# Hybrid decoder step: values of four heads in one 512-column product, gates feature-major, output projection over four open banks

## The chip, the cores and the metric

The kernel runs on one core of a Trainium2 chip. The metric is the device time of one execution in microseconds (us). Times below come from three timed runs and from one profiled execution, whose trace has every instruction of the engines: PE (TensorE, the matmuls), DVE (VectorE), ACT (ScalarE), POOL (GpSimd), and SP, which issues most DMA transfers.

## The reference, cut to what matters

One layer over 2048 prompt tokens, 16 meta tokens and 8 single-token samples, model width 1024, float32. After an RMS norm one projection with 2560 columns gives the S5 input u (512), and for four heads of 128 the query q, forget logit, value and gate (512 columns each):

```python
hn = rms_norm(h, norm_mix_g)
z = hn @ w_in                      # u | q | f | i (values) | g (gates)
y5 = s5_mix(u, ...)                # complex scan, GELU, GLU
# per head, in chunks of 64 tokens:
o = qd @ S + att @ v               # att = mask(qd @ kd^T)
S = diag(decay) @ S + kd'^T @ v
o = o * rsqrt(mean(o * o) + EPS)   # over the head's 128 columns
o = o * norm_g * silu(g)
h = h + concat([y5, o]) @ w_out
h = h + conv_ffn(rms_norm(h, norm_ffn_g), ...)
```

## The kernel before, in words

The prompt is cut into four blocks b = 0 to 3 of 512 tokens. Block 0 also carries 24 extra columns (meta tokens and samples), so its feature-major products run in two column ranges of 256 and 280. Every matrix product is made of three passes over operands split in two (`wh`, `wl` for weights, `ah`, `al` for activations): high by high, high by low, low by high. A weight unit of 1024 columns per partition is loaded into `st` (two buffers), `w_unit`; ACT copies its high part (L449) and DVE subtracts for the low one (L83); `wh` and `wl` have three buffers.

`fm_mm` (L480) makes feature-major results: weights stationary, 512 tokens wide, 24 matmuls for 128 features. `tm_mm` (L500) makes token-major results: 128 tokens stationary, 256 weight columns wide, 24 matmuls for 256 columns. `ex_mm` (L514) does the extra tokens of block 0, 16 matmuls for 256 columns.

For each block `head(b, a, h)` runs four times: the forget gate f by `fm_mm`, a chain on DVE (L612, L615, the scans L622, the reciprocal L632 and products), q by `fm_mm`, then value and gate of this head together by `tm_mm` (four row tiles, two weight units, evicted by ACT at L670 and L671), the scores (L690, masked at L693), turned keys (L696, L698), the state products (L701, L710), the outputs `po` (L713, L714), their squares on ACT (L720), the inverse root on DVE and POOL (L520, L521), a normalisation times gate on DVE for each of four row tiles (L723), four PE turnings (L726) and an ACT copy with the norm weight into `mixh` (L732).

Between the heads of block b stand S5 tiles of block b-1, `s5(b-1, ...)`, eight a block: table load L832, input products L847, rotations and scans L885 on DVE, output products L896 and L899, and after every second tile the GELU and turning (L814, L818). Block 3 has S5 tiles 0 to 3 of block 2 with head 0 and 4 to 7 with head 1, and its own with heads 2 and 3. Behind the heads come `u_proj(b)`, and for the block before it the GLU, the split of `mixh` and `out_proj`, in four column groups of 256: two weight units, 96 matmuls, addition of the residual x and a store to `h_d`. The feed-forward part follows after block 3.

The order of instructions on each engine is fixed at build time by the framework's scheduler; it may place code of one function inside another. PSUM banks come from three pools: `bank` with three for products, `gbank` with three for the heads, and two for turnings and S5.

Of the kernel before, what the change touches and what calls it, by code (L numbers as in the profile page):

```python
# [37 lines left out]
def kernel(  # L38
# [563 lines left out]
    def head(b, a, h):  # L602
# [49 lines left out]
        wu = []  # L652
        for kq in range(2):
            st = w_stage()
            for j in range(2):
                dma_w(st.rearrange("p (k j c) -> p k j c", k=4, j=2)[:, :, j],
                      ap(win, kq * 512 * 2560 + 1536 + 128 * h + 512 * j,
                         [[2560, 128], [128 * 2560, 4], [1, 128]]))
            hi, lo = split_w(st, 1024)
            wu.append((v3(hi, 4, 256), v3(lo, 4, 256)))  # L660
        v = hgp.tile([128, 4, 128], F32, name="hv")
        g = hgp.tile([128, 4, 128], F32, name="hg")
        for t2_ in range(2):
            p = v3(bank(), 2, 256)
            o = None
            for i in range(2):
                t = 2 * t2_ + i
                o = tm_mm(p[:, i, :], wu, (4, 4),
                          lambda ai, k: a[ai][:, k, t * 128:t * 128 + 128], o)
            ACT(v[:, 2 * t2_:2 * t2_ + 2], p[:, :, 0:128], AF.Copy)  # L670
            ACT(g[:, 2 * t2_:2 * t2_ + 2], p[:, :, 128:256], AF.Silu)  # L671
        if b == 0:
            pe = bank()
            ex_mm(pe[:, :256], wu, (4, 4), E["stat"], 104)
            t = ex_sum(pe, 40, 64, 256)
            ie = exa.tile([40, 256], F32, name="ie")
            add(ie, pe[:40, :256], t)
            ge = exa.tile([40, 128], F32, name="ge")
            ACT(ge, ie[:, 128:256], AF.Silu)
# [42 lines left out]
        for t in range(4):  # L722
            stt(g[:, t, :], po[:, t, :], r[:, t:t + 1], g[:, t, :], op0=OP.mult, op1=OP.mult)  # L723
        px = v3(gbank(), 4, 128)
        for t in range(4):
            nc.tensor.transpose(px[:, t, :], g[:, t, :], ident)  # L726
        if b % 2:
            mh = E["mxp"].tile([128, BT], F32, name="mixh", bufs=4)
        else:
# [245 lines left out]
    def out_proj(b, m, between=None):  # L975
# [4 lines left out]
        for q in range(4):  # L980
            if between is not None:
                between(q)
            qs = slice(256 * q, 256 * q + 256)
            wu = [w_unit(wout, 4 * kq, 4, 256 * q, 256) for kq in range(2)]
            xr = v3(x4(), 4, 256)
            dma_w(xr, x_prompt[0, b * BT:b * BT + BT, qs].rearrange("(t p) c -> p t c", p=128))
            for t2_ in range(2):
                p = v3(bank(), 2, 256)
                o = None
                for i in range(2):  # L990
                    t = 2 * t2_ + i
                    o = tm_mm(p[:, i, :], wu, (4, 4),
                              lambda ai, k: m[ai][:, k, t * 128:t * 128 + 128], o)
                add(xr[:, 2 * t2_:2 * t2_ + 2], p, xr[:, 2 * t2_:2 * t2_ + 2])
            dma(h_d[b][:, qs].rearrange("(t p) c -> p t c", p=128), xr)
            if b == 0:
                xe = scr()[:10, :256]
                dma_w(xe[0:8], x_sample.rearrange("n o d -> (n o) d")[:, qs])
                dma_w(xe[8:10], meta_tokens[14:16, qs])
                pe = bank()  # L1000
                ex_mm(pe[:, :256], wu, (4, 4), st, 42)
                t = ex_sum(pe, 10, 32, 256)
                add(t, pe[:10, :256], t)
# [265 lines left out]
```

## Time and profile before

| | us |
|---|---|
| median of three runs (2626.48 to 2635.57) | 2628.86 |
| the profiled execution | 2622.47 |
| its span in the trace | 2620.6 |
| PE busy | 2496.9 |
| DVE busy | 1456.0 |
| ACT busy | 903.6 |
| mixing part (blocks 0 to 3, to 1111.2) | 1111.2 |
| feed-forward part, from there to 2591 | 1479.8 |

Busy times are sums over the span; the engines run side by side. A chain of waits is followed back from the last instruction of a stretch. A product's time in a run is the chain's time divided by its count; the mean duration of one matmul in the groups is longer, since matmuls are pipelined.

### The profile page before, as it was taken

The numbers are of one execution on the slowest core, as the hardware profiler recorded it, in microseconds if no ns is written. First come the engines' busy times: TensorE is split into PE (matmuls) and PEld (weight loads), VectorE is DVE, ScalarE is ACT, GpSimd is POOL, SyncE is SP. The second block draws the span as 40 slices with busy tenths as digits, with TensorE's granted clock in tenths as the row PEclk, the third lists the DMA queues.
The fourth block names the chain that finished last, engine by engine and source line by source line (L and its number), as shares of the span: only waits on it lengthen the run. The fifth ranks groups of instructions, "written<-read, shape, count | busy, mean of one in ns | idle before, by whom it ended". The sixth has DMA issues, their size and how long they took to land.

```text
span 2620.6 us, 39925 instructions
## 1 busy us (share of the span) xinstructions
PE 2496.9 (95%) x16515; PEld 2263.8 (86%) x16515; DVE 1456.0 (56%) x2978; ACT 903.6 (34%) x1564; POOL 166.2 (6%) x254
## 2 busy tenths in 40 slices
PE   7887998999999999999999999999999999999998
PEld 6786876888888888989999999999889898989887
DVE  6875697678669688553333333345843333343344
ACT  3553344434425445341313131223531313131222
POOL 1232100100000001000000000000300000000000
PEclk9997999999999999999999999999999999999999
DMA  4345433553564662731111111111521111111111
GB/s 126 103 138 184 98 111 133 153 167 121 132 197 131 168 219 86 247 92 49 49 45 45 49 48 42 43 47 57 195 73 49 49 49 49 49 49 49 41 48 74
DMA packets 274939, 252.50 MB, mean 96 GB/s; under 512 B 11367, under 2 KB 255999, under 8 KB 270654
## 3 DMA queue, kind: packets, MB, share of 16 engines
q1 hardware_dynamic: 264680, 220.42, 27.9%
q0 software_dynamic: 9904, 29.48, 3.5%
q8 instruction: 129, 2.11, 0.3%
q14 instruction: 52, 0.43, 0.1%
q10 hardware_dynamic: 174, 0.06, 0.0%
HBM read 216.41 MB, written 33.27 MB: 95 GB/s over the span
## 4 chain that ended last, share of the span: by engine, by line
PE 72%; DVE 11%; ACT 4%; DMA 3%; issue 3%; POOL 1%; SPq 0%; POOLq 0%; ACTq 0%; DVEq 0%
PE mm L480 41%; PE mm L500 25%; DVE wl L83 1%; DVE hf L632 1%; PE mm L514 1%; DMA st<-in_w_out_dram 1%; POOL rstd L521 1%; DVE sB L86 1%; DMA st<-in_w_in_dram 1%; PE tp L899 1%; ACT wh L449 1%; DVE sA L885 1%; DVE al L83 1%; PE tp L847 1%; DVE sA L86 1%
## 5 line engine op out<-in xcount | busy, mean ns | idle before, releaser
L480 PE MATMUL mm<-ah,wh 128*128 128x512 f32 (+3 forms) x2320 | 817.6, 353 | 5.1 <-ACT ah L552 3.8
L480 PE MATMUL mm<-al,wh 128*128 128x512 f32 (+3 forms) x2320 | 814.6, 351 | 1.1 <-DVE al L83 1.1
L480 PE MATMUL mm<-ah,wl 128*128 128x512 f32 (+3 forms) x2320 | 814.9, 351 | 0.5 <-DVE wl L83 0.5
L449 ACT ACTIVATE wh<-st 128x1024 fp32r<-128x1024 f32 (+1 forms) x264 | 275.7, 1046 | 859.8 <-PE mm L480 315.5
L480 PEld LDWEIGHTS mm<-ah,wh 128*128 128x128 f32 x2320 | 441.1, 190 | 60.0 <-ACT ah L552 4.5
L480 PEld LDWEIGHTS mm<-ah,wl 128*128 128x128 f32 x2320 | 441.1, 190 | 55.7 <-DVE wl L83 1.0
L480 PEld LDWEIGHTS mm<-al,wh 128*128 128x128 f32 x2320 | 441.0, 190 | 54.6 <-DVE al L83 1.6
L83 DVE TENSOR_TENSOR wl<-st,wh 128x1024 fp32r<-128x1024 f32 (+1 forms) x264 | 318.1, 1206 | 272.6 <-ACT wh L449 271.4
L500 PE MATMUL mm<-wh,gh 128*128 128x256 f32 x1408 | 399.6, 284 | 2.0 <-DVE hacc L80 1.5
L500 PE MATMUL mm<-wh,gl 128*128 128x256 f32 x1408 | 399.5, 284 | 0.0
L500 PE MATMUL mm<-wl,gh 128*128 128x256 f32 x1408 | 399.2, 284 | 0.0
L500 PE MATMUL mm<-wh,ah 128*128 128x256 f32 x1024 | 291.7, 286 | 7.3 <-ACT hg L671 3.2
L500 PE MATMUL mm<-wh,al 128*128 128x256 f32 x1024 | 290.9, 284 | 5.8 <-DVE al L83 5.0
L500 PE MATMUL mm<-wl,ah 128*128 128x256 f32 x1024 | 289.0, 284 | 1.2 <-DVE wl L83 1.2
L80 DVE TENSOR_TENSOR hacc<-hacc,mm 128x512 f32<-128x512 f32 x192 | 131.3, 685 | 267.1 <-PE mm L500 267.0
L500 PEld LDWEIGHTS mm<-wh,gh 128*128 128x128 f32 x1408 | 270.9, 192 | 3.0 <-DVE hacc L80 1.7
L500 PEld LDWEIGHTS mm<-wh,gl 128*128 128x128 f32 x1408 | 270.8, 192 | 0.4
L500 PEld LDWEIGHTS mm<-wl,gh 128*128 128x128 f32 x1408 | 271.0, 192 | 0.0
L500 PEld LDWEIGHTS mm<-wh,ah 128*128 128x128 f32 x1024 | 194.7, 191 | 10.3 <-ACT hg L671 3.4
L500 PEld LDWEIGHTS mm<-wh,al 128*128 128x128 f32 x1024 | 195.2, 191 | 8.4 <-DVE al L83 6.2
L500 PEld LDWEIGHTS mm<-wl,ah 128*128 128x128 f32 x1024 | 194.8, 191 | 2.1 <-DVE wl L83 1.8
L86 DVE TENSOR_TENSOR c<-c,mm 128x512 f32<-128x512 f32 (+1 forms) x110 | 63.7, 579 | 215.6 <-PE mm L480 214.3
(377 smaller groups left out, 2606.0 us busy)
## 6 DMA issues: line engine op xcount, KB each, us to landing
st<-in_ffn_w_up_dram SPq DMA_DIRECT2D x96, 512.0 KB
big<-tab_d SPq DMA_DIRECT2D x32, 1156.0 KB
st<-in_w_in_dram SPq DMA_DIRECT2D x48, 512.0 KB
st<-in_w_in_dram SPq DMA_DIRECT2D x64, 256.0 KB
st<-in_w_out_dram SPq DMA_DIRECT2D x32, 512.0 KB
st<-in_ffn_w_down_dram SPq DMA_DIRECT2D x32, 512.0 KB
x<-in_x_prompt_dram SPq DMA_DIRECT2D x30, 512.0 KB
h_d<-x POOLq DMA_DIRECT2D x16, 512.0 KB, 4.8
```

The lines of the kernel that those rows point to most:

```text
L80: tt_(o, a, b, op=OP.add)
L83: tt_(o, a, b, op=OP.subtract)
L86: tt_(o, a, b, op=OP.mult)
L449: ACT(hi[:, :n], st[:, :n], AF.Copy)
L480: mm(p[:, :n], w[wi][:, k, :], a[ai][:, k, c0:c0 + n], start=(i == 0), stop=(i == 3 * nk - 1))
L500: o = mm(dst, lhs(ai, k), (hi, lo)[wi][:, kk, :], start=(i == 0), stop=(i == tot - 1))
L514: mm(dst[:m], stat[:, k, :m], w[:, kk, :], start=(i == 0), stop=(i == tot - 1))
L521: nc.gpsimd.tensor_tensor(r, r, mhalf[:ss.shape[0], :n], op=OP.pow)
L632: nc.vector.reciprocal(R[:, c0:c1], P[:, c0:c1])
L847: mm(pes[i // ng][:, i % ng, :], Bk[:, i, :], UT[:, i // 2, :nj], start=True, stop=True)
L885: nc.vector.tensor_tensor_scan(out=G[:, i, 1:129], data0=sv[:, RHO, g:g + 1].to_broadcast([128, 128]), data1=xr[:, i, :], initial=Hc[:, g: ...
L899: o = mm(py[:, 2 * i:2 * i + 2, :].rearrange("p a b -> p (a b)"), G[:, 2 * i + j, 0:128], Cm[:, 2 * i + j, :], start=False, stop=(j == 1))
```

## The change

Values and gates of a head are made apart. `v_proj(b)` makes the values of all four heads ahead of the block's first head: `tm_wide` keeps four banks open (two of each pool), one for each row tile of 128 tokens, takes weight units of two row blocks by 512 columns and uses each for 24 matmuls 512 wide before the next. The gate of a head is made feature-major by `fm_mm` and goes through SiLU straight into `mixh`. The normalisation of `po` becomes four ACT copies with a scale, which are turned, and one DVE instruction (L737) multiplies by norm weight and gate. `out_proj` goes through `tm_wide` too, in two groups of 512 columns. Lines of the changed kernel lie further down: L690 becomes L699, L726 becomes L735, L847 becomes L862, L538 becomes L561, L832 becomes L847.

```diff
+    def tm_wide(src, c0, lhs, done, ex=None):
+        pb = [(bank, gbank)[t % 2]() for t in range(4)]
+        pe = bank() if ex is not None else None
+        for i in range(4):
+            wu = w_unit(src, 2 * i, 2, c0, 512)
+            for t in range(4):
+                for kk in range(2):
+                    k = 2 * i + kk
+                    for j, (wi, ai) in enumerate(PASS):
+                        mm(pb[t], lhs(ai, k, t), wu[wi][:, kk, :], start=(k == 0 and j == 0),
+                           stop=(k == 7 and j == 2))
+                if i == 3:
+                    done(t, pb[t])
...
     def head(b, a, h):
...
-                dma_w(st.rearrange("p (k j c) -> p k j c", k=4, j=2)[:, :, j],
-                      ap(win, kq * 512 * 2560 + 1536 + 128 * h + 512 * j,
...
-                o = tm_mm(p[:, i, :], wu, (4, 4),
-                          lambda ai, k: a[ai][:, k, t * 128:t * 128 + 128], o)
-            ACT(v[:, 2 * t2_:2 * t2_ + 2], p[:, :, 0:128], AF.Copy)
-            ACT(g[:, 2 * t2_:2 * t2_ + 2], p[:, :, 128:256], AF.Silu)
...
+        wg = w_unit(win, 0, 8, 2048 + 128 * h, 128)
+        for p, q0, n in fm_mm(wg, a, 8, cols):
+            n_ = min(n, BT - q0)
+            ACT(mh[:, q0:q0 + n_], p[:, :n_], AF.Silu)
...
+        v = E["v"][:, :, 128 * h:128 * h + 128]
...
-            stt(g[:, t, :], po[:, t, :], r[:, t:t + 1], g[:, t, :], op0=OP.mult, op1=OP.mult)
+            ACT(ktt[:, t, :], po[:, t, :], AF.Copy, scale=r[:, t:t + 1])
...
-            nc.tensor.transpose(px[:, t, :], g[:, t, :], ident)
+            nc.tensor.transpose(px[:, t, :], ktt[:, t, :], ident)
...
-        ACT(mh[:, :BT], px.rearrange("p a b -> p (a b)"), AF.Copy, scale=ng)
+        stt(mh[:, :BT], px.rearrange("p a b -> p (a b)"), ng, mh[:, :BT], op0=OP.mult, op1=OP.mult)
...
+    def v_proj(b, a):
+        v = E["v"] = hgp.tile([128, 4, 512], F32, name="hv", bufs=1)
+        pe = tm_wide(win, 1536, lambda ai, k, t: a[ai][:, k, t * 128:t * 128 + 128],
+                     lambda t, p: ACT(v[:, t], p, AF.Copy), (E["stat"], 104) if b == 0 else None)
...
-        for q in range(4):
+        for q in range(2):
             if between is not None:
-                between(q)
+                between(2 * q)
+                between(2 * q + 1)
...
+            pe = tm_wide(wout, 512 * q, lambda ai, k, t: m[ai][:, k, t * 128:t * 128 + 128], done,
+                         (st, 42) if b == 0 else None)
...
+        v_proj(b, A[b])
         for h in range(4):
```

Where the scheduler puts this shows at three places. PE, in front of block 2 (out_proj of block 0 and head 0 of block 2). Before, the first S5 products of block 1 (L847, L896) stand ahead of a column group of the output projection (L500):

```order
L547 MATMUL tp<-ident,x_4880 128x128 x8
L547 MATMUL tp<-ident,x_4906 128x128 x8
L847 MATMUL tp<-U,big 128x128 x4
L896 MATMUL tp<-big,U 128x128
L500 MATMUL mm<-wh,ah 128x256
L500 MATMUL mm<-wh,al 128x256
L500 MATMUL mm<-wl,ah 128x256
```

After, they (now L862, L911) stand behind the last of the 96 products of `v_proj` (L518), and head 0's forget gate (L480) follows:

```order
L518 MATMUL hg<-wh,ah 128x512
L518 MATMUL hg<-wh,al 128x512
L518 MATMUL hg<-wl,ah 128x512
L862 MATMUL tp<-U,big 128x128 x4
L911 MATMUL tp<-big,U 128x128
L480 MATMUL mm<-ah,wh 128x512
L480 MATMUL mm<-al,wh 128x512
L480 MATMUL mm<-ah,wl 128x512
```

So the S5 input products moved from within the output projection to behind the values. On DVE, at the end of the first head of block 2, before (`sA`, `sB` are S5's):

```order
L715 TENSOR_SCALAR S<-S,pl 128x128
L80 TENSOR_TENSOR sB<-sB,sA 128x512
L520 TENSOR_SCALAR rstd<-ss_5829 128x4
L882 COPY sA<-Hc 128x4
L885 SCALAR_TENSOR_TENSOR sA<-sv,Hc,sB 128x128
L723 SCALAR_TENSOR_TENSOR hg<-mm,rstd,hg 128x128 x4
```

and after:

```order
L83 TENSOR_TENSOR sA<-sA,sB 128x516
L897 COPY sA<-Hc 128x4
L900 SCALAR_TENSOR_TENSOR sA<-sv,Hc,sB 128x128
L907 COPY Hc<-sA 128x4
L900 SCALAR_TENSOR_TENSOR sA<-sv,Hc,sB 128x128
L737 SCALAR_TENSOR_TENSOR mixh<-hg,vec,mixh 128x512
```

One instruction has taken the place of four, behind more of S5's work, as it waits for ACT and PE too. On SP, the loads at the end of block 0 (`x` are the token tiles of block 1's norm, `tab_d` the S5 tables), before:

```order
L459 DMA st<-in_w_in_dram 128x8x128 x2
L538 DMA x_2368<-in_x_prompt_dram 128x1024
L832 DMA big<-tab_d 128x2312
L538 DMA x_2394<-in_x_prompt_dram 128x1024
L832 DMA big<-tab_d 128x2312
L538 DMA x_2420<-in_x_prompt_dram 128x1024
L538 DMA x_2446<-in_x_prompt_dram 128x1024
```

and after:

```order
L459 DMA st<-in_w_in_dram 128x2x512 x2
L561 DMA x_2194<-in_x_prompt_dram 128x1024
L561 DMA x_2220<-in_x_prompt_dram 128x1024
L847 DMA big<-tab_d 128x2312
L561 DMA x_2246<-in_x_prompt_dram 128x1024
L561 DMA x_2272<-in_x_prompt_dram 128x1024
L847 DMA big<-tab_d 128x2312
```

A second x load passed ahead of the first table load, and two units of the value weights stand ahead of all of them.

## Rows read from the trace of the kernel before

**Rows 1.** The page's busy times: busy us, share, instructions.
```profile
PE 2496.9 (95%) x16515; PEld 2263.8 (86%) x16515; DVE 1456.0 (56%) x2978; ACT 903.6 (34%) x1564; POOL 166.2 (6%) x254
```

**Rows 2.** Windows by stage; first row names the columns.
```profile
core 0: us, PE busy (x) PEld busy (x) DVE busy (x) ACT busy (x) POOL busy (x), PEclk, DMA share, GB/s
...
60.00:245.70 185.70, 154.21 (x1086) 134.01 (x1084) 142.22 (x434) 90.15 (x219) 50.60 (x68) 0.89 0.49 145
...
545.00:700.00 155.00, 148.75 (x965) 131.48 (x965) 117.66 (x246) 65.98 (x127) 10.22 (x14) 1.00 0.40 127
...
1111.20:2591.00 1479.80, 1475.86 (x9447) 1349.42 (x9446) 621.41 (x1076) 405.88 (x587) 32.21 (x55) 1.00 0.19 57
```

**Rows 3.** Windows of one head of block 1, 2 and 3, same columns.
```profile
385.88:425.80 39.92, 38.15 (x257) 32.11 (x255) 35.89 (x104) 19.34 (x50) 1.53 (x2) 1.00 0.35 113
...
601.00:635.65 34.65, 33.54 (x230) 29.83 (x229) 30.41 (x66) 15.99 (x31) 1.64 (x2) 1.00 0.41 130
...
765.00:806.50 41.50, 37.55 (x257) 33.79 (x256) 37.12 (x76) 17.67 (x31) 1.17 (x2) 1.00 0.58 185
```

**Rows 4.** Chain of waits: start us, us, what; products in unbroken runs.
```profile
533.37 1.88 PE mm L514 x16
...
1181.60 11.51 PE mm L500 x96
...
2141.62 87.07 PE mm L480 x384
```

**Rows 5.** Groups of DVE, three heads of block 2: count, busy us, mean ns, idle.
```profile
L83 DVE TENSOR_TENSOR wl<-st,wh 128x1024 fp32r<-128x1024 f32 x12 | 14.6, 1221 | 3.9 <-ACT wh L449 3.9
L885 DVE TENSOR_TENSOR_SCAN sA<-sv,Hc,sB 128x128 f32<-128x128 f32 x24 | 10.5, 471 | 0.0
...
L86 DVE TENSOR_TENSOR sB<-tp,big 128x512 f32<-128x512 f32 x6 | 4.1, 678 | 0.0
...
L723 DVE SCALAR_TENSOR_TENSOR hg<-mm,rstd,hg 128x128 f32<-128x128 f32 x12 | 3.4, 345 | 2.6 <-POOL rstd L521 2.6
```

**Rows 6.** Chain of waits, head 1 of block 2.
```profile
598.58 0.37 ACT hv L670
...
605.42 1.13 POOL rstd L521
```

**Rows 7.** Timeline of DVE there: start us, us, engine, line.
```profile
606.57 1.13 DVE L723 SCALAR_TENSOR_TENSOR hg<-mm,rstd,hg 128x128 f32<-128x128 f32 x4 [0.84 <-POOL rstd L521]
```

**Rows 8.** Windows of blocks 1, 2 and 3, and of the last output projection.
```profile
262.80:451.60 188.80, 170.89 (x1096) 141.96 (x1094) 149.69 (x424) 84.88 (x207) 14.10 (x22) 0.98 0.40 114
535.24:676.61 141.37, 135.12 (x915) 120.39 (x914) 119.60 (x250) 61.91 (x122) 7.03 (x9) 1.00 0.45 142
766.40:863.40 97.00, 88.52 (x575) 77.09 (x573) 85.60 (x178) 45.33 (x84) 5.94 (x9) 1.00 0.52 171
766.40:882.56 116.16, 107.67 (x661) 92.98 (x660) 95.90 (x191) 54.92 (x98) 7.03 (x11) 1.00 0.55 171
...
1047.00:1084.00 37.00, 36.20 (x301) 35.63 (x301) 12.46 (x19) 6.36 (x6) 2.34 (x3) 1.00 0.86 295
```

**Rows 9.** Waits of PE from 425.8 to 451.6: us, times, longest.
```profile
PE tp L814 <- DVE sY L807: 4.5, 1, 4.5
PE tp L899 <- DVE sA L83: 3.5, 2, 3.3
```

**Rows 10.** Chain of waits at the end of block 0 and in the last projection.
```profile
226.00 5.21 DMA tab_d<-big
231.41 0.33 SPq L832
231.84 6.04 DMA x<-in_x_prompt_dram
...
1061.41 9.77 DMA st<-in_w_out_dram
```

More of the change, by code (lines that the diff above doesn't have):

```diff
@@ L505, in tm_mm @@
         return o
+    def tm_wide(src, c0, lhs, done, ex=None):
[11 more added lines that the diff above has]
+                    done(t, pb[t])
+            if ex is not None:
+                stat, m = ex
+                for kk in range(2):
+                    for j in range(2):
+                        mm(pe[:m], stat[:, 2 * i + kk, :m], wu[j][:, kk, :], start=(i + kk + j == 0),
+                           stop=(i == 3 and kk == 1 and j == 1))
+        return pe
     def ex_mm(dst, wu, nks, stat, m):
@@ L650, in head @@
         kt = f
[L652 to L655, printed above, removed]
-                dma_w(st.rearrange("p (k j c) -> p k j c", k=4, j=2)[:, :, j],
-                      ap(win, kq * 512 * 2560 + 1536 + 128 * h + 512 * j,
[L658 to L667, printed above, removed]
-                o = tm_mm(p[:, i, :], wu, (4, 4),
-                          lambda ai, k: a[ai][:, k, t * 128:t * 128 + 128], o)
-            ACT(v[:, 2 * t2_:2 * t2_ + 2], p[:, :, 0:128], AF.Copy)
-            ACT(g[:, 2 * t2_:2 * t2_ + 2], p[:, :, 128:256], AF.Silu)
-        if b == 0:
[L673 to L679, printed above, removed]
+        if b % 2:
+            mh = E["mxp"].tile([128, BT], F32, name="mixh", bufs=4)
+        else:
+            mh = hgp.tile([128, 10 + BT], F32, name="mixh", bufs=4)
+        wg = w_unit(win, 0, 8, 2048 + 128 * h, 128)
+        for p, q0, n in fm_mm(wg, a, 8, cols):
+            n_ = min(n, BT - q0)
+            ACT(mh[:, q0:q0 + n_], p[:, :n_], AF.Silu)
+            if q0 + n > BT:
+                ACT(mh[:, FM_:FS], p[:, SP - 2 - q0:SP - q0], AF.Silu)
+                ACT(mh[:, FS:FS + 8], p[:, SP - q0:W - q0], AF.Silu)
+        v = E["v"][:, :, 128 * h:128 * h + 128]
+        if b == 0:
+            ie = E["ie"][:, 128 * h:128 * h + 128]
             nc.vector.tensor_scalar(kt[:, MT:SP], kd[:, MT:SP], pl[:, 8:9], None, op0=OP.mult)
@@ L703, in head @@
             pk = gbank()
-            mm(pk[:, :128], ktm, ie[0:16, 0:128], start=True, stop=True)
+            mm(pk[:, :128], ktm, ie[0:16], start=True, stop=True)
             nc.vector.tensor_copy(S, pk[:, :128])
@@ L740, in head @@
             vbd = v3(vb, 8, 128)[32:40]
-            tt_(vbd, ie[32:40, None, 0:128].to_broadcast([8, 8, 128]),
+            tt_(vbd, ie[32:40, None, :].to_broadcast([8, 8, 128]),
                                     ident[32:40, 32:40, None].to_broadcast([8, 8, 128]), op=OP.mult)
@@ L757, in head @@
                 mm(po[:40, :128], E["qm"][:, n, :], s0v[:, n, :], start=(n == 0), stop=False)
-            mm(po[:40, :128], E["atte"], ie[0:16, 0:128], start=False, stop=True)
+            mm(po[:40, :128], E["atte"], ie[0:16], start=False, stop=True)
             ss = sm.tile([128, 1], F32, name="ss", bufs=6)
@@ L979, in out_proj, with done @@
                          [m[1][:, :, e1], m[1][:, :, e2]], 8, 10, 32)
-        for q in range(4):
+        for q in range(2):
             if between is not None:
-                between(q)
[L983 to L986, printed above, removed]
-            for t2_ in range(2):
[L988 to L995, printed above, removed]
+                between(2 * q)
+                between(2 * q + 1)
+            qs = slice(512 * q, 512 * q + 512)
+            xr = []
+            for t2_ in range(2):
+                xr.append(v3(x4(), 2, 512))
+                dma_w(xr[t2_], x_prompt[0, b * BT + 256 * t2_:b * BT + 256 * t2_ + 256, qs]
+                      .rearrange("(t p) c -> p t c", p=128))
+            def done(t, p):
+                x = xr[t // 2]
+                add(x[:, t % 2], p, x[:, t % 2])
+                if t % 2:
+                    dma(h_d[b][128 * t - 128:128 * t + 128, qs].rearrange("(t p) c -> p t c", p=128), x)
+            pe = tm_wide(wout, 512 * q, lambda ai, k, t: m[ai][:, k, t * 128:t * 128 + 128], done,
+                         (st, 42) if b == 0 else None)
             if b == 0:
-                xe = scr()[:10, :256]
+                xe = scr()[:10]
                 dma_w(xe[0:8], x_sample.rearrange("n o d -> (n o) d")[:, qs])
                 dma_w(xe[8:10], meta_tokens[14:16, qs])
[L1000 to L1003, printed above, removed]
+                t = ex_sum(pe, 10, 32, 512)
+                add(t, pe[:10], t)
                 add(xe, xe, t)
```

14 lines of the change are left out of this document (7 added, 7 removed).

## The prediction, made before the changed kernel was run

> **What bounds the kernel now.** The page's first rows make it a TensorE kernel: PE busy 95% of the span, VectorE (DVE) 56% [rows 1]. The windows by stage, read next, show that this is a mean over two kernels. From 1111.2 us on, the feed-forward part keeps PE busy 1475.9 of 1479.8 us; nothing of it is changed. The changed code lies in the first 1111 us, where DVE is close behind PE: 142.2 beside 154.2 of 185.7 us in the later heads of block 0, 117.7 beside 148.8 of 155 in block 2 [rows 2]. Third, windows of one head each: in block 2 a head takes 34.65 us with PE busy 33.5 and DVE 30.4; in block 1, whose heads carry the wider S5 work of block 0, 39.9 us with 38.2 and 35.9; the first two heads of block 3, with four S5 tiles each, 41.5 us with 37 and 37 [rows 3]. So a head is PE's by a small margin, and what is taken off PE there pays only down to DVE's time.
>
> **What the change does on PE.** Products 256 columns wide become 512 wide. The chain of waits has both in unbroken runs: 96 narrow ones in 11.51 us (119.9 ns each), 384 wide ones in 87.07 us (226.7 ns) [rows 4]. Two narrow for one wide saves 13.1 ns, and 3072 narrow ones go (1536 pairs): 20.1 us. The products of the 24 extra tokens of block 0 before: 16 narrow in 1.88 us for each of four heads and four column groups, 15.0 us. After: 16 wide for the values and 32 for the output, 10.9 us by the same pitch, and some 2.4 us for the gates of those columns, done in two ranges. With 1.7 us from there PE's own work falls by 21.8 us, 0.83% of the span. If PE decided everywhere, that would be the result.
>
> By the Trainium skill (TensorE: Matmul & The Clock Gate, Back-to-back issue gap) the isolated gap is N/2.4 + 2.5 ns, so a pair would save 2.5 ns, not 13.1, and the 1536 pairs 3.8 us. The trace differs: its pitches lie 10.7 and 10.9 ns above that formula, and the measurement decides; by the page the time would be some 16 us later.
>
> **What it does on DVE, in a head.** Gone: four normalisations of 345 ns and one of four weight splits of 1221 ns. New: one product of 128x512 out of PSUM, which has the form of the 678 ns group [rows 5]. That is 1.4 + 1.2 - 0.7 = 1.9 us a head. The splits come back as four in the values' stage, so DVE's total hardly changes. The normalisation moves to ACT as four copies; four DVE ones took 1.13 us [rows 7], and ACT's nearest, the values' eviction of twice the width, 0.37 us [rows 6], so 0.7 to 1.5 us for four: the chain from the sum of squares to the last product stays as long within 0.4 us, and ACT is busy 16 of 34.65 us [rows 3].
>
> **What it moves.** A head's PE work falls by 6.07 us (11.51 for values and gate, 24 x 0.2267 = 5.44 for the gate alone): 27.5 in block 2, below DVE's 30.4 - 1.9 = 28.5; in block 1 it is 32.1 below 34.0; in block 3, heads 0 and 1, 31.2 below 34.9. DVE becomes the bound of the heads. Against that, every block gets 96 x 0.2267 = 21.8 us of the values' products in one piece, and DVE has only four splits there. The order of PE decides what is under it: the first S5 products, which stood before and within the output projection, now stand behind the values. So the blocks must be walked one by one.
>
> Block 1, from its first forget-gate product (262.80) to the start of the GLU (451.60): 188.8 us, DVE busy 149.7 [rows 8]. PE waits at its end for the last S5 tile, 4.5 and 3.5 us [rows 9]. DVE, not PE, ends this block. After: 21.8 values, 6.0 until the first forget gate is there, 149.7 - 7.6 - 2.4 of DVE (its saving in four heads, the splits done under the values), and waits of DVE. In a head of before these are 4.0 us; since PE will be ahead I take 2.5, so 10. Sum 177.5: **-11.3** (without waits -21, with all of them and the tail's -1).
>
> Block 2, from the end of out_proj(0) (533.37 + 1.88 = 535.25, [rows 4]) to the first turning of head 3 (676.61): 141.4 us [rows 8]. After: 21.8 values, four heads at 28.5 + 1.8 of waits = 30.3, and in front of head 0 two S5 tiles that DVE had begun under the projection: four 128x512 operations and four scans of 471 ns each [rows 5], 9.6 us with the second's rest, and 1 of start. Sum 153.6, that is +12.2. PE is then some 12 wide products further into u_proj than before (-2.7), and the projection sheds those tiles' products (-2.0): **+7.5**. With heads at DVE's floor it is about 0, with 32.7 us (the 4.25 us of DVE waits of now) +17.
>
> Block 3, heads 0 and 1, from 766.40 to the last S5 turning at 863.4: 97.0 us, DVE busy 85.6 [rows 8]. After: 21.8 + 85.6 - 3.8 + 9 (two tiles' fronts, again from under the projection) + 2 of start + 9 of waits (11.4 now) = 123.6, +26.6. What follows until the next projection had 19.2 us of products; 59 wide ones, 13.4 us, stand behind that turning now: -5.8. Heads 2 and 3 have two tiles each as in block 2, where 34.65 becomes 30.3: -8.7. Sum **+12.1** (+1 to +16).
>
> Block 0: the values of all heads (96 + 16 wide, 25.4 us at full clock) stand before the first head. Every head has some 7.3 us less on PE (two ranges of 256 and 280 columns for the gate, 24 products each, 6 us by the narrow pitch, for 11.51 + 1.88). So head 0's scores come 25.4 - 7.3 = 18 us later, some 15 where the values fill waits at the start, and the later three heads can win back 22. PE was busy for 83% of that stage [rows 2]; with two thirds of the 22 gained the two cancel: **0** (-6 to +15). Its end is a chain: the table's DMA of 5.21 us, SP's table load, behind it x loads of 6.04 us, then the norm that the next block's products wait for [rows 10]. In SP's new order two x loads pass ahead of that table load, so two instead of three are left; I count nothing for it.
>
> Output projection: 384 narrow products, 46.0 us, become 192 wide, 43.5: -2.5 a block, **-10.1** in all. The same bytes are loaded; a weight load of 512 KB took 9.77 us in the last one, where the DMA engines were 86% busy and PE still 36.2 of 37 us [rows 8, 10]. A unit now feeds 5.44 us of work before the next is due.
>
> **Sum:** -11.3 + 7.5 + 12.1 + 0 - 10.1 = -1.8 us. The profiled run took 2622.47 us, so 2620.7; the median of the three runs, 2628.86, lies 6.4 above it: **2627 us**. The 21.8 us taken from PE are mostly given back as DVE time that is no longer under PE's work.
>
> **Rivals.**
> *DVE keeps up* (faster): waits of DVE nearly vanish, heads run at 28.5 and 34.0 us, block 0 gains all. For it: waits of now are partly caused by PE's own queue. Against: S5's exchanges with ACT and the POOL power (1.13 us, [rows 6]) stay. By the favourable ends, -21 + 0 + 1 - 6 - 10 = -36; half way there is 2609 us. Chance 0.29.
> *DVE's waits stay* (slower): a head of block 2 keeps 4.25 us of DVE idle, 32.7 us, and head 0 has its two tiles on top. For it: these waits stand inside a chain from DVE to PE, ACT or POOL and back. By the unfavourable ends, -1 + 17 + 16 + 0 - 10 = +22: 2650 us. It decides from about 31.5 us a head in block 2 on. Chance 0.17.
> *Block 0 is late* (slower): the setup's turnings, which make the S5 tables, stand behind head 0; if they slide by 15 us and nothing is regained, the table DMA of [rows 10] does too: +13, 2640 us. Chance 0.08.
> *It does not do what it says*: two staging buffers give a 512-column unit too late, and PE pauses between units; a load of 9.77 us against 5.44 us of work would cost 4.3 us a unit, in the last projection some 15 us: 2642. Chance 0.02, since two loads are in flight.
> *The pitch gains less*: if wide products gain only 2.5 ns a pair, 16 us of the sum are missing: 2643 us. Chance 0.01; the rows of both pitches speak against it. (That is the page's rule above.)
>
> **How the numbers follow.** What a measurement of this kernel can tell from no change is about 0.3%, 7.9 us: 2621 to 2636.7. The forecast has 0.43 for within it. Faster 0.29 is the first rival, slower 0.28 the other four. The range leaves out a tenth on each side: 2611 to 2645.
>
> **What would show it.** Heads of block 2 near 30.3 us with DVE busy 28.5 and PE 27.5; the values' stage 21.8 us with DVE busy about 5; block 1's GLU starting without the 4.5 us wait; out_proj stretches 43.5 us; narrow products gone from the groups. The forecast is wrong if PE stays over 96% busy through the heads (faster), if DVE idles over 3 us a head (slower), or if the S5 tables of block 0 come after 235 us.

## The result, and the profile after

The changed kernel takes 2644.84 us (median of seven runs, 2639.91 to 2646.56), before 2628.86 (seven runs, 2625.72 to 2635.57): a ratio of 1.006, with a 95% interval of 1.0047 to 1.0074. It is 16 us slower, where 2627 us and no change were forecast; the time lies just inside the range (2611 to 2645). The profiled execution of after took 2646.56 us, 1.7 above its median, that of before 6.4 below its own, so the two traces lie 23.9 us apart, 8 more than the medians.

The page's busy times of the changed kernel, which answer to [rows 1]:

```profile
PE 2496.9 (94%) x14995; PEld 2194.2 (83%) x14995; DVE 1444.0 (55%) x2919; ACT 909.2 (34%) x1587; POOL 168.5 (6%) x252
```

PE has 1520 matmul records fewer and the same busy time to the tenth of a us. What it was to save, 21.8 us, shows nowhere in its sum. The pitches are as forecast, though. In the chain of waits of the changed kernel (start us, us, what), one row tile's six products of the values take 1.36 us, 226.7 ns each, and the forget gate that follows has the old pitch:

```profile
276.22 1.36 PE mm L518 x6
277.58 1.36 PE hg L518 x6
278.94 5.45 PE mm L480 x24
```

Where the time went is read in windows cut at the same events in both traces. The changed kernel; columns as in [rows 2]: block 1 from the values' first product to the GLU, block 2 from the end of out_proj(0) to head 3's first turning, heads 1, 2 and 3 of block 2 (each from the turning before it to its own), the stretches of out_proj(0) and out_proj(1), block 3 from the end of out_proj(1) to the start of out_proj(2), out_proj(2), and from its end to the last head's first turning:

```profile
257.02:459.56 202.54, 178.18 (x904) 139.00 (x902) 146.36 (x412) 86.59 (x211) 13.97 (x22) 0.93 0.39 106
535.30:683.39 148.09, 135.73 (x733) 112.17 (x731) 121.20 (x250) 65.20 (x128) 8.23 (x10) 0.99 0.43 137
597.97:628.13 30.16, 27.77 (x158) 23.02 (x158) 28.22 (x62) 14.49 (x31) 1.84 (x2) 1.00 0.41 131
628.13:655.80 27.67, 25.80 (x151) 21.61 (x152) 25.97 (x55) 15.18 (x33) 1.64 (x2) 1.00 0.45 143
655.80:683.39 27.59, 24.47 (x135) 20.15 (x133) 24.03 (x51) 10.10 (x23) 1.53 (x2) 1.00 0.44 143
...
761.30:898.60 137.30, 125.40 (x642) 103.26 (x641) 103.99 (x200) 62.97 (x110) 7.24 (x11) 0.96 0.51 156
898.60:958.60 60.00, 55.66 (x265) 45.75 (x264) 38.60 (x71) 22.25 (x33) 2.12 (x3) 0.94 0.52 161
958.60:1041.50 82.90, 66.68 (x342) 54.99 (x341) 66.79 (x137) 34.78 (x67) 6.05 (x10) 0.90 0.39 128
478.20:535.30 57.10, 56.33 (x259) 42.96 (x258) 33.19 (x56) 19.89 (x32) 3.90 (x6) 1.00 0.57 177
713.90:761.30 47.40, 47.16 (x220) 38.42 (x219) 29.87 (x43) 17.64 (x25) 3.30 (x5) 1.00 0.71 206
```

The kernel before, those of the same windows that [rows 8] does not hold: out_proj(0), out_proj(1), block 3 up to out_proj(2), out_proj(2), and the last two heads:

```profile
470.28:535.24 64.96, 59.38 (x494) 57.94 (x493) 38.48 (x71) 22.45 (x38) 5.88 (x9) 1.00 0.55 160
707.10:764.40 57.30, 52.65 (x423) 50.61 (x422) 34.74 (x55) 20.12 (x29) 3.39 (x5) 1.00 0.62 180
764.40:882.56 118.16, 109.67 (x679) 94.98 (x678) 97.90 (x193) 56.29 (x100) 7.33 (x11) 1.00 0.54 168
882.56:944.20 61.64, 57.86 (x467) 55.77 (x466) 42.93 (x78) 22.77 (x34) 2.28 (x3) 1.00 0.62 189
944.20:1020.99 76.79, 72.32 (x484) 63.62 (x482) 67.36 (x139) 37.95 (x71) 6.08 (x10) 1.00 0.38 126
```

| stretch | after - before, us | forecast, us |
|---|---|---|
| block 0, to the first product of block 1 (257.02, before 262.80) | -5.8 | 0 |
| block 1 | +13.7 | -11.3 |
| out_proj(0) | -7.9 | -2.5 and -2.0 |
| block 2 | +6.7 | +12.2 and -2.7 |
| out_proj(1) | -9.9 | -2.5 |
| block 3 to out_proj(2) | +19.1 | +26.6 - 5.8 = +20.8 |
| out_proj(2) | -1.6 | -2.5 |
| heads 2 and 3 of block 3 | +6.1 | -8.7 |
| the rest | +3.5 | -2.5 |

Two rows are off by 25 and 15 us, and both contain DVE's waits. Block 1 cut into the values, head 0 and the three other heads (each to the first turning), and the tail, in the changed kernel:

```profile
257.00:279.00 22.00, 22.00 (x99) 18.23 (x98) 3.84 (x5) 5.27 (x8) 7.80 (x14) 1.00 0.93 136
279.00:324.30 45.30, 37.31 (x188) 28.75 (x186) 30.14 (x89) 17.97 (x46) 1.57 (x2) 0.89 0.28 85
324.30:357.80 33.50, 30.59 (x166) 23.32 (x167) 30.95 (x94) 17.25 (x47) 1.54 (x2) 1.00 0.37 116
357.80:395.10 37.30, 34.84 (x174) 27.99 (x174) 30.22 (x81) 15.59 (x38) 1.53 (x2) 0.86 0.25 77
395.10:430.60 35.50, 31.61 (x166) 24.56 (x165) 30.89 (x94) 17.47 (x48) 1.53 (x2) 0.95 0.34 112
430.60:459.60 29.00, 21.88 (x117) 16.22 (x117) 20.36 (x51) 13.09 (x29) 0.00 (x0) 0.93 0.39 136
```

DVE is busy 3.8 of 22 us under the values, and then idle for 15.2 us of head 0 (5.4 of them under the first forget gate), 14.2 of the other three, 8.6 of the tail. The three longest waits of DVE from 284.4 to 459.56 (us, times, longest), next to the one for the first gate, which began under the values:

```profile
DVE sB L86 <- ACT sA L273: 6.0, 8, 3.4
DVE wl L83 <- ACT wh L449: 4.9, 3, 3.4
DVE sB L86 <- ACT sY L920: 3.2, 2, 2.5
```

How head 0 loses its time stands in windows of 5 us of it:

```profile
279.00:284.00 5.00, 5.00 (x24) 4.13 (x23) 0.00 (x0) 0.58 (x1) 0.00 (x0) 1.00 0.00 0
284.00:289.00 5.00, 2.12 (x12) 1.43 (x10) 3.88 (x12) 3.17 (x6) 0.00 (x0) 0.95 0.00 0
289.00:294.00 5.00, 1.74 (x4) 1.33 (x5) 5.00 (x8) 1.73 (x5) 0.00 (x0) 0.50 0.00 0
294.00:299.00 5.00, 5.00 (x14) 3.13 (x13) 4.10 (x15) 1.54 (x4) 0.00 (x0) 0.52 0.59 175
299.00:304.00 5.00, 5.00 (x27) 3.87 (x26) 2.77 (x13) 1.06 (x1) 0.00 (x0) 1.00 0.49 143
```

and in the timeline of all engines (start us, us, instruction, in brackets the wait before it and its releaser):

```profile
287.65 3.35 DVE L655 RECIPROCAL hf<-hP 128x512 f32<-128x512 f32 x1
290.91 0.36 DVE L86 TENSOR_TENSOR sB<-tp,big 128x256 f32<-128x256 f32 x1
...
291.31 0.20 ACT L872 ACTIVATE pe<-tp 128x40 f32<-128x40 f32 x1 [3.63 <-DVE sB L86]
...
291.56 0.80 PE L911 MATMUL tp<-big,U 128*128 128x128 f32 x2 [3.89 <-ACT pe L872]
...
291.79 1.22 DVE L83 TENSOR_TENSOR wl<-st,wh 128x1024 fp32r<-128x1024 f32 x1
...
293.06 0.79 PE L480 MATMUL mm<-ah,wl 128*128 128x512 f32 x1 [0.70 <-DVE wl L83]
```

First the forget gate's products fill PE, and DVE has nothing. Then DVE works off head 0's gate, its reciprocal of 3.35 us last, and the first S5 tile, which stands in the middle of head 0's products, waits behind that: DVE's `sB`, which releases ACT's `pe`, which releases PE at L911, 3.9 us late, with the query's products (L480) queued behind. The tile is not the only thing in the way: the query's next product needs the low half of its weights, which DVE makes (`wl`, L83) behind the same reciprocal, at 291.79. From 294 on PE is full again, and behind 299 DVE has work for 2.8 of 5 us. The engines wait for each other in turn. PE's clock falls with it: from 1.00 to 0.50, that is from 2.4 to 1.2 GHz, while PE is busy 1.74 of 5 us, and it is still low under the full window behind.

Summed from windows of 10 us up to 1140 us, PE is at the lower level for 58 us before and 127 us after. In the 69 us more at that level the same products count for more busy time, which leaves room for the 21.8 us that were to be saved; this is an estimate from the windows, not a sum over products. What the level costs is read from two runs below.

### The profile page after: what moved, and what is told of

It is laid out like the page before. It is cut to its first block, busy times and chain, and to the rows that moved or that the text cites. A ratio compares the mean times of both kernels' runs of the same rounds, so it can differ in the third digit from the quotient of the medians.

```text
span 2644.5 us, 36754 instructions
## 1 busy us (share of the span) xinstructions
PE 2496.9 (94%) x14995; PEld 2194.2 (83%) x14995; DVE 1444.0 (55%) x2919; ACT 909.2 (34%) x1587; POOL 168.5 (6%) x252
## 4 chain that ended last, share of the span: by engine, by line
PE 73%; DVE 13%; issue 5%; ACT 4%; DMA 3%; POOL 1%; POOLq 0%; ACTq 0%; SPq 0%; DVEq 0%
PE mm L480 41%; PE mm L500 18%; PE mm L518 3%; PE hg L518 3%; DVE hf L655 2%; DVE sB L86 1%; DVE hP L645 1%; DVE wl L83 1%; DVE sA L900 1%; POOL rstd L544 1%; ACT wh L449 1%; PE mm L537 1%; DVE sA L86 1%; DMA h_d<-x 1%; DMA x<-in_x_prompt_dram 1%
## 5 line engine op out<-in xcount | busy, mean ns | idle before, releaser
L480 PE MATMUL mm<-ah,wh 128*128 128x512 f32 (+3 forms) x2480 | 875.4, 353 | 9.4 <-DVE hP L86 3.2
L480 PE MATMUL mm<-al,wh 128*128 128x512 f32 (+3 forms) x2480 | 874.0, 352 | 0.0
L480 PE MATMUL mm<-ah,wl 128*128 128x512 f32 (+3 forms) x2480 | 871.2, 351 | 1.7 <-DVE wl L83 1.7
L480 PEld LDWEIGHTS mm<-ah,wh 128*128 128x128 f32 x2480 | 472.6, 191 | 68.5 <-DVE hP L86 3.8
L480 PEld LDWEIGHTS mm<-ah,wl 128*128 128x128 f32 x2480 | 471.5, 190 | 60.6 <-DVE wl L83 2.2
L480 PEld LDWEIGHTS mm<-al,wh 128*128 128x128 f32 x2480 | 472.5, 191 | 56.9 <-issue 1.1
L83 DVE TENSOR_TENSOR wl<-st,wh 128x1024 fp32r<-128x1024 f32 (+1 forms) x264 | 318.5, 1207 | 338.4 <-ACT wh L449 329.2
L500 PE MATMUL mm<-wh,gh 128*128 128x256 f32 x1408 | 399.4, 284 | 2.0 <-DVE hacc L80 1.5
L500 PE MATMUL mm<-wh,gl 128*128 128x256 f32 x1408 | 399.2, 284 | 0.0
L500 PE MATMUL mm<-wl,gh 128*128 128x256 f32 x1408 | 398.9, 283 | 0.0
L500 PEld LDWEIGHTS mm<-wh,gh 128*128 128x128 f32 x1408 | 270.3, 192 | 3.0 <-DVE hacc L80 1.7
L500 PEld LDWEIGHTS mm<-wh,gl 128*128 128x128 f32 x1408 | 270.4, 192 | 0.4
L500 PEld LDWEIGHTS mm<-wl,gh 128*128 128x128 f32 x1408 | 270.4, 192 | 0.0
L1164 ACT ACTIVATE c<-c 128x512 f32<-128x512 f32 x88 | 55.6, 632 | 144.9 <-DVE c L1163 144.9
L518 PE MATMUL mm<-wh,ah 128*128 128x512 f32 x192 | 77.9, 406 | 6.7 <-ACT wh L449 6.6
L1178 ACT ACTIVATE gh<-c 128x512 fp32r<-128x512 f32 x88 | 55.0, 625 | 66.5 <-DVE c L86 65.7
L544 POOL TENSOR_TENSOR rstd<-rstd,mhalf 128x1 f32<-128x1 f32 (+3 forms) x71 | 58.2, 822 | 305.2 <-DVE rstd L543 293.4
L518 PE MATMUL mm<-wl,ah 128*128 128x512 f32 x192 | 77.1, 402 | 0.0
L518 PE MATMUL mm<-wh,al 128*128 128x512 f32 x192 | 77.0, 401 | 0.0
```

Source lines behind the costliest of these rows:

```text
L83: tt_(o, a, b, op=OP.subtract)
L480: mm(p[:, :n], w[wi][:, k, :], a[ai][:, k, c0:c0 + n], start=(i == 0), stop=(i == 3 * nk - 1))
L500: o = mm(dst, lhs(ai, k), (hi, lo)[wi][:, kk, :], start=(i == 0), stop=(i == tot - 1))
L518: mm(pb[t], lhs(ai, k, t), wu[wi][:, kk, :], start=(k == 0 and j == 0), stop=(k == 7 and j == 2))
L544: nc.gpsimd.tensor_tensor(r, r, mhalf[:ss.shape[0], :n], op=OP.pow)
L1164: ACT(c, c, AF.Silu)
```

## Experiments

Ratios are to the kernel before on the same chip, with 95% intervals; the changed kernel has 1.0060.

**Each half alone.** The first takes the kernel before and changes out_proj only; the second takes the changed kernel and puts the old out_proj back.

```diff
# e1_out_wide, from the kernel before
-        for q in range(4):
+        for q in range(2):
...
+            pe = tm_wide(wout, 512 * q, lambda ai, k, t: m[ai][:, k, t * 128:t * 128 + 128], done,
# e2_values_only, from the changed kernel: the reverse
```

> The kernel before with the output projection alone changed (two groups of 512 columns over four open banks). Theory: between the two kernels the stretches of out_proj became 7.8, 9.9 and 1.6 us shorter and the last part 3.4 us longer, 16 in sum, and all of the loss is in the heads and the values. Then this kernel is 10 to 16 us faster than before, about 2615. Rival: the out_proj stretches became shorter only because S5 tiles and their waits left them for the heads; then the gain is that of PE's work alone, 5 us or less, 2624 or later.

> The changed kernel with the output projection of before (four groups of 256 columns); values of four heads at once and feature-major gates as changed. Theory: the loss of some 40 us in the blocks (13.7 in block 1, 6.7 in block 2, 19.1 and 6.1 in block 3, less 5.8 in block 0) belongs to this part, so 2655 to 2670. Rival, that a part of it comes from the output projection's order: 2650 or earlier.

Measured: the projection alone 2617.01 us, ratio 0.9961 (0.9947 to 0.9975), 10 us faster; the values and gates alone 2645.38 us, 1.0065 (1.0043 to 1.0088). The first lies on the theory's side of the two (about 2615, 2624). The second missed: 2655 at least was expected, and it lies on the rival's side (2650 or earlier). The halves do not add: the projection is worth 10 us on the kernel before and nothing behind the values. The windows of e1_out_wide show where the time goes (out_proj(0), out_proj(1), out_proj(2), and from there to the last head's first turning):

```profile
470.20:525.70 55.50, 54.72 (x248) 41.67 (x247) 31.78 (x52) 19.02 (x29) 3.88 (x6) 1.00 0.63 179
699.70:747.20 47.50, 47.39 (x220) 38.45 (x219) 29.82 (x43) 17.64 (x25) 3.31 (x5) 1.00 0.70 206
866.20:925.90 59.70, 55.79 (x265) 45.84 (x264) 38.61 (x71) 22.29 (x33) 2.11 (x3) 0.94 0.53 161
925.90:1010.80 84.90, 75.36 (x493) 66.15 (x493) 70.78 (x146) 38.46 (x72) 6.39 (x11) 0.98 0.43 137
```

The free-standing stretches are 9.5 and 9.8 us shorter: PE's work by 4.7 and 5.3, and its waits, 5.6 and 4.7 us before, are down to 0.8 and 0.1. But the two heads behind out_proj(2) take 84.9 instead of 76.8 us.

**Why out_proj(2) costs the heads behind it.** It has S5 tiles of block 3 between its groups; with two wide groups two tiles are called ahead of each.

```diff
# e8_out_wide_but_block2, from e1_out_wide (out_proj_n is the old out_proj)
-        out_proj(b, M[b], between)
+        (out_proj_n if between is not None else out_proj)(b, M[b], between)
```

> The kernel before with the wide output projection in blocks 0, 1 and 3, and the projection of block 2, which has S5 tiles of block 3 between its column groups, in four groups of 256 as before. With all four wide the time was 9 us below before; its windows show 10 us gained in each of the first two and 6 us lost from out_proj(2) to the last head. Theory: two calls of the S5 tile ahead of each wide group leave DVE and PE waiting in turn; with four groups there the 6 us come back, 2608 to 2614. Rival: the loss there came from elsewhere, 2615 to 2619 as with all four wide.

Measured: 2614.66 us, 0.9954 (0.9938 to 0.9970), between the two expectations. The windows (out_proj(2); the heads behind it):

```profile
867.00:929.50 62.50, 57.53 (x467) 55.65 (x466) 42.88 (x78) 22.76 (x34) 2.28 (x3) 1.00 0.61 184
929.50:1006.40 76.90, 72.41 (x485) 63.74 (x484) 67.46 (x140) 37.94 (x71) 6.13 (x10) 1.00 0.39 127
```

The heads are back at 76.9 us, for 2.8 us more in the projection: 5.2 us. The time moved by 2, inside the intervals. The windows show the place; the clearer test of the times is the last pair below.

**Values made head by head.**

```diff
# e3_values_per_head, from the changed kernel
-        v_proj(b, A[b])
...
+        wv = w_unit(win, 0, 8, 1536 + 128 * h, 128)
...
+        for t in range(4):
+            o = tm_mm(pv[:, t, :], [wv], (8,), lambda ai, k: a[ai][:, k, t * 128:t * 128 + 128], o)
```

> The changed kernel, but each head makes its own values again, 128 columns wide in one weight unit, behind its gate; gates feature-major, normalisation on ACT and output projection as changed. Theory: the loss comes from the values in one piece of 22 us, under which DVE has four splits only; then this is faster than the changed kernel by 20 us or more and near before, 2610 to 2630, though 128-column products cost PE more. Rival: the heads lose by the longer end of their chain (ACT copies, turning, one DVE product); then it stays at 2640 or above.

Measured: 2785.78 us, 1.0598 (1.0574 to 1.0621), neither expectation. In its chain of waits 91 of these products take 10.11 us:

```profile
681.20 10.11 PE mm L500 x91
```

That is 111 ns for 128 columns, beside 119.9 for 256 [rows 4]: halving the width saves 7%, so a head's values alone cost almost what values and gate together did. It says nothing on the chain and was no fit test of it.

**S5 tiles ahead of the values.** Two, and four, tiles of the block before are called ahead of `v_proj`.

```diff
# e4_two_tiles_ahead (e5_four_tiles_ahead: (0, 1, 2, 3)), from the changed kernel
+        if b > 0:
+            s5(b - 1, U[b - 1], M[b - 1], (0, 1))
         v_proj(b, A[b])
...
```

> The changed kernel with the first two S5 tiles of each block ordered ahead of the values, so that their fronts lie within out_proj and the values' products in blocks 2 and 3. Theory, DVE idle under the values: 8 to 15 us faster than the changed kernel in blocks 2 and 3, nothing in block 1, where the S5 input is not there yet: 2630 to 2637. Rival, that the heads' own chain sets the time: within 4 us of 2645.

> The changed kernel with four S5 tiles of the block before ordered ahead of the values of blocks 1 to 3, the rest with every second head. Two tiles ahead gave some 12 us. Theory (DVE idle under the dense stretches decides): four tiles ahead give 5 to 15 us more, 2618 to 2628. Rival (only the fronts of two tiles fit there, buffers and the finishing steps hold the rest back): as with two, 2630 to 2636, or later, since tiles are bunched in the heads.

Measured: two tiles 2633.0 us, 1.0023 (1.0012 to 1.0034), some 10 us back, as expected; four tiles 2652.0 us, 1.0093 (1.0070 to 1.0116), worse than none. In the trace of the second the first S5 turning of block 2 comes at 559.8 us, in the changed kernel at 582.7; but head 3's first turning stands at 684.0, there at 683.4. The tiles moved and the block did not get shorter; why the total got longer was not followed up.

**Work for PE in the heads.**

```diff
# e6_filler, from the changed kernel, behind the gate, blocks 1 to 3
+            pd = bank()
+            for i in range(12):
+                mm(pd, wg[0][:, i % 8, :], a[0][:, i % 8, 0:BT], start=True, stop=True)
+            nc.vector.tensor_copy(junk[:, :2], pd[:, :2])
```

> The changed kernel with 12 products of 128x512 that nobody needs (a DVE copy of two columns reads them) behind the gate of each head of blocks 1 to 3: 12 x 12 x 0.2267 = 32.6 us more work for PE, in front of the scores, where PE now waits for DVE. Theory: in these heads PE is ahead of DVE, and its waits cost more than their length, since the granted clock falls to 1.2 GHz in them; then the fillers lie in the waits, the clock of the heads stays higher, and the time moves by -8 to +8 us. Rival, PE's work decides in the heads: +25 to +33 us.

Measured: 2642.94 us, 1.0059 (1.0042 to 1.0077): with 32.6 us more of PE's work the total does not move. But its parts do. Heads 1, 2 and 3 of block 2, and the stretch behind out_proj(2):

```profile
596.40:624.10 27.70, 27.15 (x155) 22.76 (x155) 24.69 (x54) 13.44 (x29) 1.64 (x2) 1.00 0.44 143
624.10:655.00 30.90, 30.04 (x169) 25.09 (x169) 29.00 (x63) 14.70 (x31) 1.64 (x2) 1.00 0.39 129
655.00:685.60 30.60, 28.68 (x154) 23.55 (x154) 25.66 (x54) 12.19 (x27) 1.53 (x2) 1.00 0.39 129
...
958.80:1036.60 77.80, 66.97 (x364) 55.11 (x364) 66.58 (x140) 34.63 (x67) 6.80 (x10) 0.98 0.41 136
```

In block 2, where the clock is 1.00 in both kernels, the three heads take 89.2 us instead of 85.4: some 3.8 us for 8.2 us of added work, so PE has room there for about half of it. In the last stretch the time falls from 82.9 to 77.8 us with more work, and the clock rises from 0.90 to 0.98. From 250 us on PE is at 1.2 GHz for 31 us instead of 75. The fillers' cost and a gain from the clock may thus cancel, and this run does not show that the lower clock is free.

**What the lower clock costs.** In block 1, behind the values, e2_values_only and the changed kernel run the same instructions in the same order on PE, DVE and ACT. Heads 2 and 3 of the changed kernel are in the table of block 1 above; those of e2:

```profile
352.10:387.10 35.00, 32.34 (x175) 25.75 (x175) 30.34 (x81) 15.63 (x38) 1.53 (x2) 0.95 0.27 84
387.10:421.30 34.20, 30.30 (x165) 23.32 (x165) 30.90 (x94) 17.47 (x48) 1.53 (x2) 1.00 0.35 116
```

DVE's work is equal (61.1 and 61.2 us), but the two heads take 72.8 us in the changed kernel and 69.2 in e2. At 0.86 and 0.95 the changed kernel's PE is at the lower level for 13.7 us of them, e2's for 3.4: 3.6 us for 10.3 us, or 0.35 us for each. The timed runs point the same way: over the 55 runs of the kernel before that stand beside the experiments, each us more at the lower level (twice the missing share of the clock, times the run's length) goes with 0.39 us more time, correlation 0.83. A correlation alone would not tell cause from effect; the two heads, with one order and one amount of work, say more. The changed kernel's median clock is 0.975 and that of these 55 runs 0.985, some 53 us more at the lower level. At 0.35 to 0.39 that is an estimated 19 to 21 us, as much as the whole loss of 16. So PE's waits cost twice, by their length and by the clock that falls in them.

**Tiles of block 1 one head later.**

```diff
# e7_block1_later, from the changed kernel
+            elif b == 1:
+                if h:
+                    s5(0, U[0], M[0], ((), (0, 1, 2), (3, 4, 5), (6, 7))[h])
```

> The changed kernel with the S5 tiles of block 1 one head later in the program: none with head 0, three with head 1, three with head 2, two with head 3. In the changed kernel the first turning of head 0 comes 45 us behind the values, since DVE takes tile 0 first and the scores wait for its chain. Theory: that is what makes block 1 long; head 0 ends 10 to 13 us earlier and the block 4 to 10 us, 2635 to 2641. Rival, block 1 is set by DVE's sum and by the last tile's tail: no change, or later, 2643 to 2655.

Measured: 2650.54 us, 1.0088 (1.0069 to 1.0108), the rival's side. Head 0's first turning came at 318.2 instead of 324.3, but the last S5 turning of the block at 463.4 instead of 456.9 (block 1 began 2.0 us later). Taking the tile out of head 0's way moves DVE's work to the block's end.

**How much of the values lies bare, and what PE's work in a head was worth.** Both leave products out.

```diff
# e9_few_value_products, from the changed kernel: 16 of 96 products of the values
+                        if few and (kk, j) != ((0, 0) if i < 3 else (1, 2)):
+                            continue
...
# e10_third_of_value_gate, from the kernel before: 8 of 24 products of each row tile
+                    if not few or i % 24 in (0, 4, 8, 12, 16, 20, 22, 23):
...
```

> The changed kernel with 16 of the 96 products of the values in each of blocks 1 to 3 (weights, splits, evictions and loads as they were); 80 x 0.2267 = 18.1 us of PE's work are left out per block, 54.4 in all, so the values are wrong. Theory: the values' stage lies bare on the path, with DVE idle under it; 45 to 55 us faster than the changed kernel, 2590 to 2600. Rival: part of it covers the weight loads, the first splits and the S5 input's way through memory; then less than 30 us, 2615 or later.

> The kernel before with 32 of the 96 value and gate products in each head of blocks 1 to 3, all else as it was; 64 x 0.1199 = 7.7 us of PE's work less per head, 92 us in all, so values and gates are wrong. Theory: in a head DVE stands 3 to 4 us behind PE, so a head of block 2 falls from 34.65 to 30 to 32 us, and of the 92 us some 35 to 50 come back: 2577 to 2592. Rival, PE decides in the heads: 75 to 92 us, 2535 to 2552.

Measured: e9 2612.12 us, 0.9935 (0.9914 to 0.9956): of 54.4 us some 33 come back, between the two expectations. e10 2621.75 us, 0.9972 (0.9961 to 0.9984): of 92 us only 6 to 7 come back, far from both. One head of block 2, one of block 1, and block 1's tail in e10:

```profile
612.80:644.10 31.30, 27.47 (x167) 23.87 (x168) 28.67 (x64) 15.91 (x32) 1.85 (x2) 0.95 0.42 135
327.00:365.70 38.70, 31.48 (x174) 25.55 (x174) 33.07 (x91) 17.82 (x45) 1.53 (x2) 0.87 0.36 116
406.50:457.60 51.10, 32.66 (x155) 23.93 (x155) 34.11 (x102) 19.09 (x43) 0.00 (x0) 0.76 0.29 100
```

The head of block 2 did fall to 31.3 us, as the theory had it. Block 1 gave back what its heads won: the tail is 51.1 us, where it was 26.6 before. The scheduler had put the instructions in another order, so this is not the old order with less work; but with 92 us less for PE the block's last S5 turning came 8.7 us later (457.6, before 448.9). PE's work in this run is not 92 us less in time, though: its busy time from 250 to 1140 us fell by 62 us (770.0, before 832.1), as it was at the lower level for 102 us there, before for 10. At 0.35 us each the clock alone may have eaten some 32 us, so what the 92 us are worth at one clock stays open, and the theory's 35 to 50 us is not refuted.

**Values behind the first head's forget gate and query.** If DVE starves since everything it could do stands behind the values, it should help to let head 0 begin first.

```diff
# e11_values_after_q, from the changed kernel, in head(), behind the query's products
+        if h == 0:
+            v_proj(b, a)
         wg = w_unit(win, 0, 8, 2048 + 128 * h, 128)
...
-        v_proj(b, A[b])
# e12_values_after_q_mix: the same, with the out_proj of e8
```

> The changed kernel with the values of the four heads made inside head 0, behind its forget gate and query and ahead of its gate, instead of ahead of the head. Leaving 54.4 us of these products out brought 33 us, so three fifths of them lie bare on the path. Theory: DVE is idle under them because head 0's own chain (forget gate, scans, reciprocal) and the S5 tile start only behind them; with f and q first, 20 to 35 us of the four stages are covered, and the kernel is faster than both, 2608 to 2624. Rival: the heads behind simply take DVE's time wherever the values stand, 2635 to 2645.

> The same with the output projection of block 2 in four groups of 256 columns and the other three wide. Theory: the two pieces add, 2 to 6 us less than with all four wide. Rival: no difference within 2 us.

Measured: 2624.91 us, 0.9985 (0.9973 to 0.9998), and 2617.6 us, 0.9957 (0.9942 to 0.9972). Moving the same products behind two others is worth 20 us, with PE at the lower level for 44 us from 250 us on instead of 75. Windows of e11: block 1 up to the first product of out_proj(0), block 2 and block 3 as above:

```profile
258.00:471.70 213.70, 193.95 (x1033) 153.04 (x1031) 158.76 (x438) 97.50 (x232) 19.41 (x30) 0.96 0.40 110
527.20:671.80 144.60, 134.83 (x738) 111.33 (x735) 121.69 (x251) 65.42 (x128) 8.23 (x10) 1.00 0.43 142
749.80:876.50 126.70, 121.06 (x642) 98.91 (x641) 104.07 (x200) 62.70 (x110) 7.84 (x11) 1.00 0.54 169
```

Against the changed kernel (222.0 by the same cut, 148.1 and 137.3) they are 8.3, 3.5 and 10.6 us shorter, with the same DVE work. And the old projection in block 2 brings 7 us more, the intervals just clear of each other: the price of two tiles ahead of each wide group.

Three versions come out at the same time, 10 to 12 us below the kernel before: the wide projection alone, the same without block 2 (0.9954, the lowest), and e12. None of them shows a gain from the values of four heads.

## Why the prediction was wrong

*The pitches* were right: 226.7 ns, 13.1 ns saved a pair, as measured again. By the formula for the isolated gap in the Trainium skill (TensorE: Matmul & The Clock Gate, Back-to-back issue gap) a pair would have saved 2.5 ns; the pitches here, 119.9 and 226.7 ns, differ from it.

*DVE bounds the heads after the change*: right in part in block 2. A head was forecast at 30.3 us with DVE at 28.5; head 1 has 30.16 with 28.22, but heads 2 and 3 have 27.67 and 27.59 with 25.97 and 24.03, so the mean is 28.5 us, beside 34.65 [rows 3]. PE, busy 27.8, 25.8 and 24.5 us, is as close to the heads' length as DVE, and e6_filler shows that it has room for about half of 8.2 us more. The 2.7 us that PE was to be ahead in u_proj did not come: from head 3's first turning to out_proj(1) both kernels take 30.5 us. (In block 3 the sums 31.2 and 34.9 should be 31.5 and 35.2 by [rows 3]; nothing rests on that.)

*The values in one piece are not covered*: right in kind. DVE was to have four splits under them and has 3.8 us of work. Block 3 was forecast at +20.8 and measured +19.1. e9 and e11 confirm it from two sides: 33 us of 54 come back when the products go, 20 when they stand behind the first head's query, part of the latter perhaps by the clock.

*Block 1, -11.3 us, is the step that failed, in the term for DVE's waits: 10 us for four heads and the tail.* DVE's work was right (147 us by the sum, 146.4 measured), and so, nearly, was its idle time under the values and the first forget gate (20.5 us by the sum, 18.2 + 5.4 = 23.6 measured). Behind them DVE is idle for 32.6 us instead of 10: 9.8 in the rest of head 0, 14.2 in the three other heads, 8.6 in the tail. Three things were missing in the 10. Head 0 was taken to begin like any other; but DVE can begin on its gate only behind the values, works it off up to the reciprocal, and the split and the S5 tile that PE needs next stand behind that. The tail was put at nothing, though its wait stood in the trace of before [rows 9], and it stands there unchanged:

```profile
456.86 1.11 PE L829 MATMUL tp<-ident,sY 128*128 128x128 f32 x4 [4.45 <-DVE sY L822]
```

And the clock was left out: behind the first forget gate PE is at the lower level for 27.7 us of block 1, in the whole block before for 7.0; at 0.35 us each that is an estimated 7 of the 25 us by which the block missed. How much each of the three adds by itself is not separated. That PE's lead would shorten the waits inside the heads, from 4.0 us to 2.5, was not wrong as such: where the clock stayed at 1.00, in head 1 of the changed kernel and head 3 of e2, DVE is idle for 2.6 and 3.3 us; where it fell to 0.86 and 0.95, in heads 2 and 3 of the changed kernel, for 7.1 and 4.6. And the heads did pay: the three behind the first turning take 35.4 us each, beside 39.9 in a head before [rows 3] and 36.5 forecast (34.0 and 2.5 of waits). The block lost its time ahead of that turning, which came 67.3 us behind the block's start (before 31.8), and the 21.4 us won back up to head 3's did not cover that.

*Heads 2 and 3 of block 3, -8.7 us*, failed for another reason, which the prediction had not looked for: out_proj(2), with two tiles ahead of each wide group. Without it (e2, clock 0.98) the same stretch is 71.7 us, 5.1 shorter than before; with it 82.9, at 0.90.

*The projection, -10.1 us*, was too small for the two free stretches (-7.9 and -9.9): the waits in it, 5.6 and 4.7 us before and 0.8 and 0.2 after, went too, and I had counted PE's work only. *Block 0*, forecast as even, came 5.8 us earlier.

The rival that came true is "DVE's waits stay" (2650 us, chance 0.17), though not at its place: it put the waits into block 2 (+17, measured +6.7) and left block 1 at -1, where +13.7 was measured. That its 2650 us lies near the measured time is luck. "Block 0 is late" and "the pitch gains less" did not happen.

Open remains why the two halves, 10 us gained and 17 lost, give 16 lost together; some 5 to 8 us of it are out_proj(2), which e12 shows. Open too is how the loss divides between the waits and the clock that falls in them, since no run holds the clock while the waits stay.

## What to carry to other kernels

Work taken from a stretch pays there at most down to the next engine's time: heads of block 2 fell from 34.65 to 28.5 us when 6 us of PE's work left each. But see what it does where it goes. When products are gathered into one dense piece, ask first what the other engines can do meanwhile, and put the piece behind whatever starts their chains: the same 96 products of each block cost 20 us less in all a few instructions later. A wait that ends a block in the trace of before belongs in the sum at full length, unless a row shows what would end it sooner. And before reading what added or left-out products were worth, compare the granted clock of the two runs: it can hide the answer, as in e6 and e10.

## What was not expected of the hardware

Products 128 columns wide cost 111 ns, beside 119.9 for 256 and 226.7 for 512 in the same kind of pass. And the lower clock costs time even where PE waits for other engines: the same instructions in the same order took 3.6 us longer with 10.3 us more at 1.2 GHz (heads 2 and 3 of block 1, the changed kernel against e2).
